# Seven-product FFN blocks for all 22 blocks of a hybrid decoder step, with no FFN block beside the sampled tokens

## The chip, the core and the metric

The kernel runs on one NeuronCore of a Trainium2 chip. The metric is the device time of one execution in microseconds (us). The engines are PE (TensorE, matrix products), DVE (VectorE), ACT (ScalarE), POOL (GpSimd) and SP (SyncE, which here only issues transfers). PE writes its results to PSUM banks; DVE or ACT read them from there. Each engine works through its own instructions in a fixed order, and so does each queue of transfers.

## What is computed

One layer of a decoder for a prompt of 1024 tokens and for 8 x 8 sampled tokens that have a past of 4096, 1024 channels wide, in float32. The token-mixing half has a short convolution, a dilated attention with six heads and a windowed attention. What matters here:

```
def apply_layer(x, mod, mixer, g_mix, g_ffn, w_out, w_gate_up, w_down):
    shift1, scale1, gate1, shift2, scale2, gate2 = mod
    mix, states = mixer(rmsnorm(x, g_mix) * (1 + scale1) + shift1)
    x = x + gate1 * (mix @ w_out)
    x = x + gate2 * swiglu(rmsnorm(x, g_ffn) * (1 + scale2) + shift2, w_gate_up, w_down)
    return x, states

def swiglu(h, w_gate_up, w_down):
    gate, up = jnp.split(h @ w_gate_up, 2, axis=-1)
    return (jax.nn.silu(gate) * up) @ w_down
```

The sampled tokens attend to a cache of 2048 keys and values for each of the 8 batches. The updated windows of these caches are outputs too, so most of the cache is copied from DRAM to DRAM as well.

## The kernel before

**Layout.** Channels lie on the 128 partitions, tokens on the free axis: 1088 columns, the prompt's 1024 and the sampled 64. The columns are split into three groups (`GRP`): 366, 366 and 356 columns; the sampled tokens are the end of the third. The FFN has 2816 hidden channels, 22 blocks of 128. A block needs a gate and an up product, 1024 channels deep each.

**Three matmuls for one.** float32 operands are split into a rounded high part and the rest (`halves` for weights, L85 to L93; `split_mix`, `second_norm` and `split_hid` for activations). `mm3` (L199) multiplies high by high, high by rest and rest by high. So a product of one block, one group and half the depth (512 channels, four chunks of 128) is 4 x 3 = 12 matmuls, and a full gate or up product of one group is 24. These are what the text calls large matmuls. ACT makes a weight's high part (L90), DVE or POOL its rest (L91).

**Seven products (Strassen's way, in Winograd's form).** `gate_up_2x2` (L968) treats gate and up for groups 0 and 1 as a 2 x 2 block product: weights are cut by gate/up and by half of the depth, activations by group and by half of the depth. Eight half-depth products become seven (7 x 12 = 84 large matmuls in place of 96). For that it needs four weight combinations for each block (t1 to t4, L972 to L975 on POOL) and, once for all blocks, four combinations of the activations, SA[1] to SA[4] (`sums_step`, L955, called four times: per call four additions on POOL, four on DVE, and the split of four results on ACT and DVE). Group 2 has no partner and stays at its 48 matmuls for a block. Before, 16 of the 22 blocks, 4 to 19, are done this way.

**Order of the work.** The program is written in stages; a scheduler then fixes each engine's order.
1. Modulation, norm, input projection, prompt attention.
2. The sampled tokens (`sample_steps`, L714): first three pairs of query heads of the windowed attention, then three pairs of heads of the dilated one, here called the first, second and third pair. Each of these streams 10 loads of 512 KB of keys and 10 of values from the cache (`stream_in`, L650), through seven buffers. Between its steps stands other work (`ahead_steps`, L879): the convolution projections, the output projection `w_out` (L754) for groups 0 and 1, their second norm, and FFN blocks 0 to 3 for groups 0 and 1 in the plain form (`gate_up`, L829, and `down_steps`, L860), with one modulation tile (`late_mod`, L355: four loads of 256 KB, 8 + 2 small matmuls) after each block. In FFN blocks 0 to 3 and in stage 1 state copies from DRAM to DRAM are issued on ACT's queue (`next_copy`, L103).
3. Pool `mid` (L915): the split of group 2's mix, `w_out` for group 2, its norm, and blocks 20 and 21 in the plain form for groups 0 and 1.
4. Pool `ffn` (L928): group 2 of blocks 0 to 3 with the four `sums_step` calls between them, their down product for group 2, group 2 of blocks 20 and 21 and their down products, then blocks 4 to 19 in pairs: two `gate_up_2x2`, then the down products of the pair. The last pair's down products are done by other column ranges (`LAST`), each followed by the final norm and the output transfers.

Group 2's output projection needs the sampled tokens' mix of all heads in the second half of its depth. PSUM has three buffers of the kind `ps_g`, which projections and down products use. Weights arrive in five buffers `wraw` and are split into four buffers `wsp`, all loaded by SP's one queue.

Of the kernel before, what the change touches and what calls it, by code (L numbers as in the profile page):

```python
# [15 lines left out]
KC = 8  # L16
# [14 lines left out]
FF_GROUPS = ((0, 4), (20, 2)) + tuple((f, 2) for f in range(4, 20, 2))  # L31
# [32 lines left out]
def _build(nc, tc, d, cst, rows, actp, stream, psum):  # L64
# [708 lines left out]
    def tmp():  # L773
        if "ff" in scratch:
# [85 lines left out]
    def down_steps(f0, hid, gs):  # L860
        if len(hid) == 4:
            for m in range(KC):
                w = wsel(split(d["w_dn"][f0 // 4, m]))
                for g in gs:
                    down(w, m, GRP[g], hid)
                yield
            return
        for q in range(4):
            w = wsel(split(d["w_d2"][f0 // 2 - 2, q]))
# [9 lines left out]
    def ahead_steps():  # L879
# [16 lines left out]
        flat = act_tile().rearrange("p h k c -> p (h k c)")  # L896
        hid = [flat[:, f * 1464:f * 1464 + 1464].rearrange("p (h c) -> p h c", h=2)
               for f in range(4)]
        for f0, nf in FF_GROUPS[:1]:
            for f in range(nf):  # L900
                gate_up(f0 + f, row("u_ff"), hid[f], (0, 1))
                late_mod(1)
                yield
            yield from down_steps(f0, hid[:nf], (0, 1))
# [7 lines left out]
    late_mod(16)  # L912
    samp.close()
    FE = FF_GROUPS[1][0]
    with tc.tile_pool(name="mid", bufs=1) as mid:  # L915
        scratch["ff"] = mid
        state["sub"] = 0
        mx[2] = mid.tile([128, 2, KC, 366], F32R, name="mx2")
        split_mix(2, mx[2])
        for m in range(KC):  # L920
            w_out(m, (2,))
        second_norm(2, second_rstd(2))
        first = [row("u_ff") for _ in range(NPRE)]
        for f, u in enumerate(first):
            gate_up(FE + f, u, None, (0, 1))

    early_pool.close()
    with tc.tile_pool(name="ffn", bufs=1, reuse_waits="tile") as ff:  # L928
        sums = ExitStack()
        sp_ = sums.enter_context(tc.tile_pool(name="sums", bufs=1, reuse_waits="tile"))  # L930
        scratch["ff"] = ff

        def hid_tile():
            return ff.tile([128, 2, T], F32R, tag="hid", bufs=2, name="hid")

        def tw():
            return sp_.tile([128, 512], F32, tag="tw", bufs=4, name="tw")
# [3 lines left out]
        N2 = GRP[0][1]  # L941
        SA = {i: sp_.tile([128, 2, 4, N2], F32R, name=f"sa{i}") for i in (1, 2, 4)}
        SA[3] = h2[1][:, :, 0:4, :]

        def whole(src, k):
            t = tw()[:, :N2]
            G.tensor_tensor(t, src[:, 0, k, :].bitcast(F32), src[:, 1, k, :].bitcast(F32), op=OP.add)
            return t

        def keep(i, k, t):  # L950
            hi, lo = SA[i][:, 0, k, :], SA[i][:, 1, k, :]
            S.activation(hi, t, AF.Copy)
            V.tensor_tensor(lo, t, hi.bitcast(F32), op=OP.subtract)

        def sums_step(k):  # L955

            a21, a22, a11 = whole(h2[1], k), whole(h2[1], k + 4), whole(h2[0], k)
            V.tensor_tensor(a22, a21, a22, op=OP.add)
            keep(1, k, a22)
            V.tensor_tensor(a21, a11, a21, op=OP.subtract)  # L960
            keep(3, k, a21)
            V.tensor_tensor(a11, a22, a11, op=OP.subtract)
            keep(2, k, a11)
            a12 = whole(h2[0], k + 4)
            V.tensor_tensor(a12, a12, a11, op=OP.subtract)
            keep(4, k, a12)

        def gate_up_2x2(f, hh):  # L968
            c2, n2 = GRP[2]
            b11, b12, b22, b21 = [load(d["w_gu"][f, n, hf]) for n, hf in ((0, 0), (1, 0), (1, 1), (0, 1))]  # L970
            t1, t2, t3, t4 = [tw() for _ in range(4)]
            G.tensor_tensor(t1, b12, b11, op=OP.subtract)  # L972
            G.tensor_tensor(t2, b22, t1, op=OP.subtract)
            G.tensor_tensor(t3, b22, b12, op=OP.subtract)
            G.tensor_tensor(t4, b21, t2, op=OP.subtract)  # L975
            u, uv = row("u"), row("uv")
            u2, u3 = uv[:, 0:N2], uv[:, N2:2 * N2]
            g0, g1, g2 = [u[:, c:c + n] for c, n in GRP]

            def product(ps, w, a, first):  # L980
                mm3(ps, w, [(k, k) for k in range(4)], a, N2, first=first, more=not first)

            def third(ps, w, half, first):
# [3 lines left out]
            w = wsel(halves(b11))  # L987
            pa, pg = ps_tile("s"), ps_tile("g")
            product(pa, w, lambda hl, k: h2[0][:, hl, k, :], True)
            S.activation(u2, pa[:, :N2], AF.Copy)  # L990
            third(pg, w, 0, True)
            pb = ps_tile("t")
            product(pb, wsel(halves(t2)), lambda hl, k: SA[2][:, hl, k, :], True)
            V.tensor_tensor(u2, u2, pb[:, :N2], op=OP.add)
            pd = ps_tile("s")
            product(pd, wsel(halves(t3)), lambda hl, k: SA[3][:, hl, k, :], True)
            V.tensor_tensor(u3, u2, pd[:, :N2], op=OP.add)
            w = wsel(halves(b21))
            product(pa, w, lambda hl, k: h2[0][:, hl, 4 + k, :], False)
            S.activation(g0, pa[:, :N2], AF.Silu)  # L1000
            third(pg, w, 1, False)
            ins = S.activation(g2, pg[:, :n2], AF.Silu)
            pe = ps_tile("t")
            product(pe, wsel(halves(t1)), lambda hl, k: SA[1][:, hl, k, :], True)
            V.tensor_tensor(u3, u3, pe[:, :N2], op=OP.add)
            product(pd, wsel(halves(t4)), lambda hl, k: h2[1][:, hl, 4 + k, :], False)
            V.tensor_tensor(g1, u2, pd[:, :N2], op=OP.add)
            S.activation(g1, g1, AF.Silu)
            V.tensor_tensor(g1, g1, u3, op=OP.mult)
            split_hid(u, hh, N2, N2)  # L1010
            w = wsel(halves(b22))
            product(pe, w, lambda hl, k: SA[4][:, hl, k, :], False)
            V.tensor_tensor(u2, u2, pe[:, :N2], op=OP.add)
            V.tensor_tensor(g0, g0, u2, op=OP.mult)
# [5 lines left out]
            split_hid(u, hh, c2, n2)  # L1020
            next_copy(ins)


        c2, n2 = GRP[2]
        for f0, nf in FF_GROUPS[:1]:
# [190 lines left out]
```

## Time and profile before

| | |
|---|---|
| median of 3 runs | 1411.46 us (1411.25 to 1416.62) |
| the profiled execution | 1411.32 us |
| its span, first to last instruction | 1409.5 us |
| PE busy, matmuls | 1353.3 us (96%), 9097 |
| DVE busy | 841.0 us (60%) |
| ACT busy | 582.5 us (41%) |
| POOL busy | 329.1 us (23%) |
| mean granted clock of PE | 0.982 |
| bytes moved by DMA | 190.81 MB |

A row of the profile names the line, the engine, the operation and the tiles (out<-in), then the time. `ps_` tiles are in PSUM, `wraw` is a loaded weight, `wsp` a split one, `raw` a piece of the cache, `tw` a scratch tile of the sums. A matmul's own duration overlaps with that of the next one, so its price is taken from the distance of starts: the number of matmuls in a window in which PE never waits.

### The profile page before, as it was taken

The page shows a single profiled execution, that of the slowest core. Times are in us where ns is not written, and L with a number is a line of the kernel's source. Part 1 is how long each engine was busy: PE and PEld are TensorE (multiplying, and loading weights), DVE is VectorE, ACT ScalarE, POOL GpSimd, SP SyncE. Part 2 cuts the span into 40 slices and gives each one's busy share as a digit, 9 for nine tenths or more (in the row PEclk, how much of TensorE's full clock was granted, in tenths as well). Part 3 has the DMA queues.
Part 4 walks back from the last instruction along what each step waited for, and adds up shares of the span by engine and source line. Part 5 has one row for each costly group of instructions (what it writes and reads, how often), then busy time and mean ns, then how long its engine had stood idle before and what let it go on. Part 6 is the DMA issues. An engine that isn't in the chain of part 4 may idle for free.

```text
span 1409.5 us, 23915 instructions
## 1 busy us (share of the span) xinstructions
PE 1353.3 (96%) x9097; PEld 1286.7 (91%) x9097; DVE 841.0 (60%) x1935; ACT 582.5 (41%) x1204; POOL 329.1 (23%) x364
## 2 busy tenths in 40 slices
PE   7999999999999998998998999999999999999994
PEld 5889999979898887888998999999999999999994
DVE  5468768265775326214569665757565666665657
ACT  5398764465654325222344413131313232322243
POOL 2143343233335220102015020202021111111114
PEclk9999999999999999999999999999999999999997
DMA  9342421452416679875333513141515142423103
GB/s 361 107 160 99 135 99 29 128 191 90 143 31 218 208 251 331 280 253 169 112 123 103 143 45 120 30 165 45 186 31 187 51 159 68 144 87 130 44 30 128
DMA packets 100804, 190.81 MB, mean 135 GB/s; under 512 B 14048, under 2 KB 51456, under 8 KB 100096
## 3 DMA queue, kind: packets, MB, share of 16 engines
q1 hardware_dynamic: 94112, 135.67, 30.1%
q10 hardware_dynamic: 6416, 53.55, 10.6%
q8 instruction: 72, 1.18, 0.3%
q14 instruction: 44, 0.36, 0.1%
q0 software_dynamic: 160, 0.04, 0.0%
HBM read 181.22 MB, written 59.23 MB: 171 GB/s over the span
## 4 chain that ended last, share of the span: by engine, by line
PE 83%; DMA 7%; DVE 4%; issue 2%; POOL 1%; ACT 1%; SPq 0%; POOLq 0%; ACTq 0%; DVEq 0%
PE ps_g L205 18%; PE ps_g L207 18%; PE ps_g L206 18%; PE ps_s L206 3%; PE ps_s L205 3%; PE ps_s L207 3%; DMA wraw<-in_w_gu 3%; PE ps_o L579 3%; PE ps_t L206 2%; PE ps_t L205 2%; PE ps_t L207 2%; PE ps_t L570 2%; DMA raw<-in_bv 1%; PE ps_g L180 1%; PE ps_s L528 1%
## 5 line engine op out<-in xcount | busy, mean ns | idle before, releaser
L205 PE MATMUL ps_g<-act,wsp 128*128 128x366 f32 (+1 forms) x1192 | 400.0, 337 | 5.5 <-ACT wsp L90 3.3
L207 PE MATMUL ps_g<-act,wsp 128*128 128x366 f32 (+1 forms) x1192 | 396.0, 333 | 4.0 <-DVE wsp L91 3.9
L206 PE MATMUL ps_g<-act,wsp 128*128 128x366 f32 (+1 forms) x1192 | 397.7, 334 | 0.4 <-DVE act L617 0.4
L90 ACT ACTIVATE wsp<-wraw 128x512 fp32r<-128x512 f32 x232 | 145.3, 629 | 270.5 <-PE ps_g L207 170.4
L205 PEld LDWEIGHTS ps_g<-act,wsp 128*128 128x128 f32 x1192 | 227.6, 191 | 13.0 <-issue 5.5
L207 PEld LDWEIGHTS ps_g<-act,wsp 128*128 128x128 f32 x1192 | 227.1, 191 | 9.2 <-DVE wsp L91 5.0
L91 DVE TENSOR_TENSOR wsp<-wraw,wsp 128x512 fp32r<-128x512 f32 x194 | 144.5, 745 | 146.3 <-ACT wsp L90 141.5
L206 PEld LDWEIGHTS ps_g<-act,wsp 128*128 128x128 f32 x1192 | 227.8, 191 | 4.0 <-issue 2.5
L205 PE MATMUL ps_g<-hid,wsp 128*128 128x366 f32 (+3 forms) x464 | 152.7, 331 | 4.6 <-DVE ts L767 3.6
L206 PE MATMUL ps_g<-hid,wsp 128*128 128x366 f32 (+3 forms) x464 | 152.3, 328 | 1.7 <-DVE hid L852 1.7
L207 PE MATMUL ps_g<-hid,wsp 128*128 128x366 f32 (+3 forms) x464 | 152.6, 329 | 0.0
L972 POOL TENSOR_TENSOR tw<-wraw 128x512 f32<-128x512 f32 x16 | 21.8, 1365 | 322.9 <-DMA wraw<-in_w_gu 157.0
L205 PEld LDWEIGHTS ps_g<-hid,wsp 128*128 128x128 f32 x464 | 87.6, 189 | 7.2 <-issue 3.6
L90 ACT ACTIVATE wsp<-tw 128x512 fp32r<-128x512 f32 x64 | 40.5, 633 | 122.5 <-PE ps_g L207 59.3
L206 PE MATMUL ps_s<-act,wsp 128*128 128x366 f32 x272 | 90.2, 332 | 0.0
L205 PE MATMUL ps_s<-act,wsp 128*128 128x366 f32 x272 | 90.1, 331 | 0.0
L206 PEld LDWEIGHTS ps_g<-hid,wsp 128*128 128x128 f32 x464 | 87.9, 189 | 2.5 <-DVE hid L852 2.3
L207 PE MATMUL ps_s<-act,wsp 128*128 128x366 f32 x272 | 89.9, 330 | 0.0
L91 POOL TENSOR_TENSOR wsp<-wraw,wsp 128x512 fp32r<-128x512 f32 x38 | 49.9, 1313 | 169.6 <-ACT wsp L90 158.0
L207 PEld LDWEIGHTS ps_g<-hid,wsp 128*128 128x128 f32 x464 | 87.8, 189 | 0.0
L763 DVE SCALAR_TENSOR_TENSOR p_qc<-ps_g,MOD,p_qc 128x366 f32<-128x366 f32 (+3 forms) x99 | 56.5, 572 | 39.9 <-PE ps_g L207 38.0
L763 DVE SCALAR_TENSOR_TENSOR p_q<-ps_g,MOD,p_q 128x366 f32<-128x366 f32 (+3 forms) x99 | 55.3, 570 | 38.5 <-PE ps_g L207 38.5
(346 smaller groups left out, 2453.3 us busy)
## 6 DMA issues: line engine op xcount, KB each, us to landing
wraw<-in_w_gu SPq DMA_DIRECT2D x112, 256.0 KB, 2.7
wraw<-in_wmod SPq DMA_DIRECT2D x64, 256.0 KB, 3.6
raw<-in_bk SPq DMA_DIRECT2D x30, 512.0 KB, 7.8
raw<-in_bv SPq DMA_DIRECT2D x30, 512.0 KB, 8.4
out_bk_b<-in_bk ACTq DMA_DIRECT2D x12, 1016.0 KB, 7.3
wraw<-in_w_in SPq DMA_DIRECT2D x36, 256.0 KB, 5.4
wraw<-in_w_d SPq DMA_DIRECT2D x36, 256.0 KB, 2.6
mraw<-in_wmod SPq DMA_DIRECT2D x32, 256.0 KB, 5.2
```

The source lines that it names most:

```text
L90: S.activation(sp[:, 0, :], raw, AF.Copy)
L91: (V if not state["sub"] or state["n"] % state["sub"] else G).tensor_tensor(sp[:, 1, :], raw, sp[:, 0, :].bitcast(F32), op=OP.subtract)
L180: ins = PE.matmul(ps[32 * q:32 * q + 32, :256], lhsT=csil[:, 4 * hf + q, :], rhs=raws[2 * hf + q // 2][:, q % 2 * 256:q % 2 * 256 + 256], ...
L205: PE.matmul(ps[:, :n], lhsT=w_hi, rhs=a(0, ak), start=first and j == 0, stop=False, **kw)
L206: PE.matmul(ps[:, :n], lhsT=w_hi, rhs=a(1, ak), start=False, stop=False, **kw)
L207: PE.matmul(ps[:, :n], lhsT=w_lo, rhs=a(0, ak), start=False, stop=last and j == m - 1, **kw)
L528: PE.matmul(ps[:, :sn], lhsT=QH[:, qsl], rhs=KS[hd][:, kk], start=True, stop=False)
L570: PE.transpose(pt[:, col:col + 128], Sb[:, (kb - k0) * 128:(kb - k0 + 1) * 128], ident)
L579: PE.matmul(po[:, q0:q0 + w], lhsT=Vt[:, kb, hd].rearrange("p a b -> p (a b)"), rhs=PT[:, hl, c0:c0 + w], start=fresh, stop=ch is chunks[- ...
L763: ins = V.scalar_tensor_tensor(x1[m][:, c0:c0 + k], ps[:, :k], MOD[:, gate + m, 0:1], x1[m][:, c0:c0 + k], op0=OP.mult, op1=OP.add)
L972: G.tensor_tensor(t1, b12, b11, op=OP.subtract)
```

## The change

All 22 blocks are done with seven products, and no FFN block stands beside the sampled tokens any more.

```
-FF_GROUPS = ((0, 4), (20, 2)) + tuple((f, 2) for f in range(4, 20, 2))
+FF_AHEAD = ()
+FF_PAIRS = (20,) + tuple(range(0, 20, 2))
...
         for m in range(KC):
             w_out(m, (0, 1))
+            late_mod(m % 2)
             yield
...
-        for f0, nf in FF_GROUPS[:1]:
-            for f in range(nf):
+        for f0 in FF_AHEAD:
...
+    mx[2] = act_tile()
+    split_mix(2, mx[2])
     samp.close()
...
-        mx[2] = mid.tile([128, 2, KC, 366], F32R, name="mx2")
-        split_mix(2, mx[2])
         for m in range(KC):
             w_out(m, (2,))
+            if m % 2:
+                sums_step(m // 2)
         second_norm(2, second_rstd(2))
         first = [row("u_ff") for _ in range(NPRE)]
         for f, u in enumerate(first):
-            gate_up(FE + f, u, None, (0, 1))
+            gate_up_2x2(FE + f, u, None)
...
-            next_copy(ins)
+        for _ in range(2 if f < 6 or hh is None else 1):
+            next_copy(ins)
```

- Blocks 20 and 21 come first for groups 0 and 1, now with seven products; `gate_up_2x2` takes the result row from its caller and leaves out group 2 where it gets no `hh` tile. Blocks 0 to 3 join the pairs. `down_steps` knows only pairs now, and the weights of all pairs lie in one array `w_dn`.
- The four modulation tiles that were left stand after every second block of `w_out`.
- Group 2's mix is split into a third big activation tile before the sampled tokens' pool is closed; the four `sums_step` calls stand between group 2's `w_out` blocks, and the pool of the sums is open until the end. The last norm's scratch lies in the memory of SA[1].
- The state copies that stood at blocks 0 to 3 go to the seven-product blocks: two at blocks 0 to 5 and in front for 20 and 21, one at the others.

The lines after L761 have moved by a few numbers in the new file: L655 there is the cache load of L653, L940 to L947 are the additions of the sums on DVE (L958 to L965 before), L935 the split of a sum (L953), L929 its additions on POOL (L947).

SP's queue, from the second pair's last values to the seventh of the third pair's values, before (`in_bk` are keys, `in_bv` values, `in_w_gu` FFN weights, `in_wmod` modulation weights):

```order
L653 DMA raw<-in_bv 128x4x256 x6
L653 DMA raw<-in_bk 128x4x256 x7
L97 DMA wraw<-in_w_gu 128x512 x3
L97 DMA wraw<-in_wmod 128x512 x4
L97 DMA wraw<-in_w_gu 128x512 x4
L97 DMA wraw<-in_wmod 128x512 x2
L653 DMA raw<-in_bk 128x4x256 x3
L97 DMA wraw<-in_wmod 128x512 x2
L97 DMA wraw<-in_w_gu 128x512
L653 DMA raw<-in_bv 128x4x256 x7
```

The same queue after, from the second pair's last keys on (`in_w_out` are the projection's weights, `in_xT` the third group's columns of the input):

```order
L99 DMA wraw<-in_w_out 128x512 x6
L655 DMA raw<-in_bk 128x4x256 x3
L655 DMA raw<-in_bv 128x4x256 x4
L99 DMA wraw<-in_w_out 128x512 x2
L655 DMA raw<-in_bv 128x4x256 x6
L655 DMA raw<-in_bk 128x4x256 x10
L759 DMA cv<-in_xT 128x356 x2
L759 DMA p_q_2101<-in_xT 128x356
L655 DMA raw<-in_bv 128x4x256
L759 DMA p_q_3212<-in_xT 128x356
```

Before, FFN and modulation weights stand between the third pair's loads; after, its keys follow the second pair's values at once, and its values stand behind the input's columns. From the first pair's first value to the second pair's last there were nine weight loads, and there are seventeen.

DVE's queue around the first of the sums, before (`act` is SA[3], which lies in an activation tile; `u_ff` is a row of block 20 or 21):

```order
L91 TENSOR_TENSOR wsp<-wraw,wsp 128x512
L958 TENSOR_TENSOR tw<-tw 128x366
L91 TENSOR_TENSOR wsp<-wraw,wsp 128x512
L960 TENSOR_TENSOR tw<-tw 128x366
L953 TENSOR_TENSOR sa_8244<-tw,sa_8244 128x366
L836 TENSOR_TENSOR u_ff<-u_ff,ps_g 128x366
L962 TENSOR_TENSOR tw<-tw 128x366
L953 TENSOR_TENSOR act<-tw,act 128x366
```

and after (`mixS` is the sampled tokens' mix, `cv` the first row of the projection's result; L765 and L769 are its evacuation):

```order
L708 COPY mixS<-ps_t 64x4x8 x4
L623 TENSOR_TENSOR act<-mixS,act 128x64
L940 TENSOR_TENSOR tw<-tw 128x366
L942 TENSOR_TENSOR tw<-tw 128x366
L935 TENSOR_TENSOR sa_6761<-tw,sa_6761 128x366
L944 TENSOR_TENSOR tw<-tw 128x366
L935 TENSOR_TENSOR act<-tw,act 128x366
L765 SCALAR_TENSOR_TENSOR cv<-ps_g,MOD,cv 128x292
L769 TENSOR_TENSOR ts<-ps_g,MOD 128x64
L947 TENSOR_TENSOR tw<-tw 128x366
L93 TENSOR_TENSOR wsp<-wraw,wsp 128x512
```

Before, the sums share DVE with blocks 0 to 3 and 20 and 21; after, they begin right behind the last copy of the sampled tokens' mix, and the projection's first evacuation stands behind five of them.

More of the change, by code (lines that the diff above doesn't have):

```diff
@@ L927, in _build @@
-    early_pool.close()
[L928 to L983, printed above, removed]
@@ new lines, in gate_up_2x2, with product, third @@
+    def gate_up_2x2(f, u, hh):
+        c2, n2 = GRP[2]
+        b11, b12, b22, b21 = [load(d["w_gu"][f, n, hf]) for n, hf in ((0, 0), (1, 0), (1, 1), (0, 1))]
+        t1, t2, t3, t4 = [tw() for _ in range(4)]
+        G.tensor_tensor(t1, b12, b11, op=OP.subtract)
+        G.tensor_tensor(t2, b22, t1, op=OP.subtract)
+        G.tensor_tensor(t3, b22, b12, op=OP.subtract)
+        G.tensor_tensor(t4, b21, t2, op=OP.subtract)
+        uv = row("uv")
+        u2, u3 = uv[:, 0:N2], uv[:, N2:2 * N2]
+        g0, g1, g2 = [u[:, c:c + n] for c, n in GRP]
+        def product(ps, w, a, first):
+            mm3(ps, w, [(k, k) for k in range(4)], a, N2, first=first, more=not first)
+        def third(ps, w, half, first):
+            if hh is not None:
@@ L1013, in gate_up_2x2 @@
[L1013 to L1014 removed]
+        w = wsel(halves(b11))
+        pa = ps_tile("s")
+        pg = ps_tile("g") if hh is not None else None
+        product(pa, w, lambda hl, k: h2[0][:, hl, k, :], True)
+        S.activation(u2, pa[:, :N2], AF.Copy)
+        third(pg, w, 0, True)
+        pb = ps_tile("t")
+        product(pb, wsel(halves(t2)), lambda hl, k: SA[2][:, hl, k, :], True)
+        V.tensor_tensor(u2, u2, pb[:, :N2], op=OP.add)
```

158 lines of the change are left out of this document (89 added, 69 removed).

## The prediction

> **What bounds the kernel now.** I read the page first, then the busy time by stage, then the tiles that mark where a stage begins, and last the queues of SP and DVE at two places.
>
> ```profile
> span 1409.5 us, 23915 instructions
> PE 1353.3 (96%) x9097; PEld 1286.7 (91%) x9097; DVE 841.0 (60%) x1935; ACT 582.5 (41%) x1204; POOL 329.1 (23%) x364
> PE 83%; DMA 7%; DVE 4%; issue 2%; POOL 1%; ACT 1%; SPq 0%; POOLq 0%; ACTq 0%; DVEq 0%
> ```
>
> PE is busy in 96% of the span and is 83% of the chain that ended last. So a product taken away is worth its time, as long as something is there to fill PE wherever it waits for a transfer. To see where that is, I cut the span at the first sampled scores, at the first product of the third group's output projection and at the first product after it that belongs to pair 20, 21 for the third group. The tiles give the first two cuts:
>
> ```profile
> L661 PE MATMUL ps_s<-raw,Q x288: 278/379/647, 450.7 to 595.6; 128*32 128x256 f32 x96, 128*32 128x136 f32 x24, 128*32 128x264 f32 x24
> L205 PE MATMUL ps_g<-mx,wsp x64: 320/325/329, 679.3 to 710.2; 128*128 128x356 f32 x64
> ```
>
> and the windows give each stage (columns: length, then busy time and count of PE, PEld, DVE, ACT, POOL, clock, DMA share, GB/s):
>
> ```profile
> 450.70:679.30 228.60, 214.25 (x1946) 189.83 (x1946) 80.82 (x194) 72.09 (x140) 39.46 (x58) 0.96 0.74 244
> 679.30:797.70 118.40, 114.35 (x686) 113.20 (x685) 85.76 (x186) 54.01 (x104) 28.52 (x29) 0.99 0.41 123
> 797.70:1409.50 611.80, 590.97 (x3546) 587.11 (x3544) 387.65 (x757) 181.71 (x329) 106.53 (x86) 0.99 0.29 98
> ...
> 975.00:1000.00 25.00, 25.00 (x153) 25.00 (x152) 15.83 (x30) 8.00 (x15) 3.83 (x3) 1.00 0.37 126
> ```
>
> The last row is plain FFN with the seven products: PE never idle, DVE at 63%, one product each 25.00 / 153 = 0.1634 us. The first row is another world: DMA is busy 74% of it, because the sampled tokens' keys and values stream through, and PE keeps going only because four FFN blocks lie beside them. The change takes exactly that cover away.
>
> **Saving: 11.8 us.** Six blocks (0 to 3, 20, 21) go from eight products of two groups to seven. One product is 12 matmuls, so 6 x 12 = 72 matmuls x 0.1634 = 11.8 us of PE. Down products stay the same in number; two pairs in place of one four-block group add 24 evacuations to DVE, hidden at 63%.
>
> The three stages hold 878, 672 and 3504 large matmuls by the program's order before, and 338, 324 and 4320 after (the sum falls by 72). Up to 450.7 us PE's order is the same in both, so I build the new time stage by stage from there.
>
> **Third stage.** 816 matmuls more than before at 0.1634 are 133.3 us: 611.8 + 133.3 = 745.1 us. The tail is the same work in other memory, costed at nothing. Of the 26 state copies on ACT's queue eight were beside the four FFN blocks of the sampled stage; they move into the second and third stage, where at a DMA share of 0.29 they are hidden.
>
> **First stage, A: when PE can go on with the third group's projection.** That needs the last sampled pair's output, so it needs its last values. Rows on the transfers:
>
> ```profile
> wraw<-in_wmod SPq DMA_DIRECT2D x64, 256.0 KB, 3.6
> raw<-in_bk SPq DMA_DIRECT2D x30, 512.0 KB, 7.8
> raw<-in_bv SPq DMA_DIRECT2D x30, 512.0 KB, 8.4
> ...
> wraw<-in_w_out SPq DMA_DIRECT2D x32, 256.0 KB, 2.7
> ...
> p_qc<-in_xT SPq DMA_DIRECT2D x3, 178.0 KB, 3.6
> ...
> raw<-in_cck SPq DMA_DIRECT2D x2, 256.0 KB, 4.4
> ```
>
> ```profile
> 446.70 3.07 SPq L653 DMA_DIRECT2D raw<-in_bk  x3
> 503.77 9.72 SPq L653 DMA_DIRECT2D raw<-in_bk  x7
> 542.38 9.65 SPq L653 DMA_DIRECT2D raw<-in_bk  x7
> ```
>
> ```profile
> 455.00:480.00 25.00, 25.00 (x276) 21.84 (x276) 8.86 (x27) 8.18 (x19) 8.37 (x16) 1.00 0.43 137
> ...
> 520.00:525.00 5.00, 5.00 (x40) 4.59 (x42) 2.24 (x4) 1.50 (x3) 0.00 (x0) 1.00 0.32 98
> 545.00:550.00 5.00, 5.00 (x65) 4.57 (x61) 3.69 (x8) 3.05 (x7) 0.00 (x0) 1.00 1.09 360
> ...
> 645.00:650.00 5.00, 5.00 (x37) 4.76 (x40) 0.60 (x1) 0.00 (x0) 0.00 (x0) 0.62 0.31 111
> ```
>
> ```profile
> 549.45 1.67 PE ps_o L695 x56
> ...
> 618.01 0.30 PE ps_g L207
> ...
> 649.06 0.17 PE ps_g L207
> ...
> 654.68 0.22 PE ps_t L701 x2
> ```
>
> When the queue is full it moves 360 GB/s. Before, the second pair's values are used up at 551 (549.45 + 1.67), and the third pair's first seven key loads have been issued at 542.38; the rest of that pair then waits behind FFN weights until 650. Now SP's queue has nothing of the FFN in between. From the first pair's first value to the second pair's last it carries 17 weight loads of 256 KB where it carried 9, 2.1 MB more, 5.8 us at 360 GB/s: 554 is my time for that point, a little less than 551 + 5.8, because the transfers had pauses there (below). Behind it come 20 loads of 512 KB, eight of 178 KB and three of 256 KB, 12.7 MB, 35.4 us: 589.5. From the last value to the split copy of the output there are products, an eviction, two transposes, four copies and a split. Before, L701 followed the products by 4 us with other work in between, and I take 4.5 us for the whole. A = 594.
>
> The four modulation tiles that used to lie beside the FFN blocks move into the first two groups' projection. Their matmuls and copies are the same; their 16 loads now stand on SP's queue in front of the first pair's keys and values. Up to 480 the transfers are busy 43% of the time, so the bytes (4.2 MB, 12 us) fit there. But a load of these needs one of five weight buffers, held until PE has used the tile before, and the keys are queued behind it: that is one reason for the upper bound below. The split of the third group's mix (16 copies on ACT, as many subtractions on DVE and POOL) moves ahead of the last pair and is hidden by PE's waiting; only its last column block is in the 4.5 us.
>
> Bounds of A: all 43.1 MB that SP is given from the first sampled load on (60 loads of 512 KB, 39 of 256, 8 of 178), at 360 GB/s without a pause, end 120 us after 446.70 and give A = 571. If the third pair's round takes as long as the second did (503.77 to 549.45, 45.7 us) and starts only at 554, its end is 600, and with xT and projection weights ahead of its values and the chain behind, A = 610. PE has 338 large matmuls (55 us) and the sampled products in 143 us, so it idles. Its clock falls in pauses (0.62 in the window at 645, products 0.30 apart at 618 and 0.17 at 649). That costs up to 3 us after a pause; I count it as covered by what follows.
>
> **Second stage, B: projection, sums and two blocks.** The sums for the seven products (L940 to L948, 16 additions on POOL, 16 on DVE, 16 splits) used to lie beside third-group products of four blocks; now they lie beside the projection, and DVE has them in its queue ahead of the projection's evacuations: PE, with three PSUM buffers for it, waits whenever an evacuation stands behind a sum. What they did before:
>
> ```profile
> 740.00:776.00 36.00, 32.14 (x184) 31.25 (x183) 33.65 (x53) 17.62 (x35) 18.76 (x15) 0.95 0.34 102
> ```
>
> ```profile
> 740.53 1.30 DVE L958 TENSOR_TENSOR tw<-tw 128x366 f32<-128x366 f32 x1 [2.07 <-POOL tw L947]
> 741.76 1.46 DVE L91 TENSOR_TENSOR wsp<-wraw,wsp 128x512 fp32r<-128x512 f32 x1
> 743.13 0.53 DVE L960 TENSOR_TENSOR tw<-tw 128x366 f32<-128x366 f32 x1
> ...
> 747.85 0.68 DVE L91 TENSOR_TENSOR wsp<-wraw,wsp 128x512 fp32r<-128x512 f32 x1
> ...
> 787.19 0.52 DVE L763 SCALAR_TENSOR_TENSOR cv<-ps_g,MOD,cv 128x292 f32<-128x292 f32 x1 [3.36 <-PE ps_g L207]
> 787.63 0.21 DVE L767 TENSOR_TENSOR ts<-ps_g,MOD 128x64 f32<-128x64 f32 x1
> ```
>
> DVE was busy 33.65 of 36 us and PE got 184 matmuls where 36 / 0.1634 would be 220. In the new place DVE holds 32 sums and splits at 0.53 (17.0 us), 10 weight splits at 0.68 (6.8) and 8 evacuations at 0.52 + 0.21 + 0.21 (7.5): 31.3 us. To that come the long forms (1.30 for 0.53, 1.46 for 0.68; ten such as before, 7.5 us) and POOL's first two additions: 41 us. PE has 156 matmuls (25.5 us) until then; the 168 matmuls of blocks 20 and 21 need the last sums and follow with 27.5 us. B = 68, beside a bare PE time of 324 x 0.1634 = 52.9, the lower bound. The third group's norm lies beside those 168.
>
> The upper bound of B comes from the long forms. In the rows below POOL's additions took from 0.962 to 3.249 us, and DVE's, with two inputs in SBUF, 0.53 or 1.30.
>
> ```profile
> L947 POOL TENSOR_TENSOR tw<-act x16: 962/1204/3249, 738.6 to 768.7; 128x366 f32<-128x366 f32 x16
> L958 DVE TENSOR_TENSOR tw<-tw x4: 526/910/1302, 740.5 to 766.9; 128x366 f32<-128x366 f32 x4
> ```
>
> Should the two engines take turns throughout, POOL's 16 x 0.962 = 15.4 us stand in place of my 7.5: B = 76. I keep 68, since most of DVE's rows stayed at 0.53. The Trainium skill's page "SBUF — State Buffer", section "Who interferes with whom", says that a DVE instruction with two SBUF inputs and a GpSimd instruction that reads SBUF exclude each other, and that the second blocks until the first is through. By that rule the sum is 1417 and not 1409; the trace agrees in part, with 1.30 for some and 0.53 for most.
>
> **The sum.** 594 + 68 + 745.1 = 1407.1 us of span. The profiled execution reports 1411.32 us, 1.8 more than its span, and the median of the three runs is 1411.46: I forecast 1409. Taken apart: beside its large matmuls at 0.1634 the first stage held 228.6 - 143.5 = 85.1 us, and will hold 143.3 - 55.2 = 88.1; the second 118.4 - 109.8 = 8.6, and will hold 68 - 52.9 = 15.1. These 9.5 us more are set against the 11.8 us saved.
>
> **The rivals.** About 0.5% (7 us) is what a measurement here can tell from no change: 1404.4 to 1418.5 is "same".
>
> 1. Forecast, both losses as priced: 1403 to 1418. Chance 0.34.
> 2. Faster: SP's queue has no FFN load and ACT's no state copy in the sampled stage any more, so the stream runs nearer its own floor. A = 583, half way between 571 and 594, and the sums find PE less bare, B = 64: 1394. For it: 1.09 DMA share at 545. Against: seven buffers hold the loads back. It decides below A + B = 657. Chance 0.34.
> 3. Slower: the third pair's keys, softmax and values come one after another as the second's did, with nothing for PE: A = 610, B = 68, 1425. For it: that round took 45.7 us before. Against: 36 projection matmuls and the split copies run beside it. It decides above A = 603. Chance 0.24.
> 4. POOL and DVE take turns in the sums: B = 76, 1417, at the upper edge of "same". Chance 0.05.
> 5. The change does not do what it says: a block of seven products is no cheaper, because its sums on DVE and POOL bind. Then 11.8 us are missing: 1421. Against: PE at 25.00 of 25.00 in the row at 975. Chance 0.03.
>
> **How the numbers follow.** Faster is case 2, 0.34. Same is cases 1 and 4 less a sliver, 0.38. Slower is cases 3 and 5 and that sliver, 0.28. The range takes in case 2 with its spread and most of case 3: 1389 to 1426.
>
> **What would show it.** In the new profile: the first projection product after the sampled tokens near 594 (case 2 near 583, case 3 near 610); PE's busy time from 450 to there well under its length with the DMA share over 0.8; DVE above 90% for some 40 us behind it, and the first pair product 20 some 41 us after; then 745 us to the end, with 153 matmuls per 25 us. Should the third stage be longer than 750, the moved work costs more than I say. Should PE's matmul count fall by other than 72, the saving is wrong.

## The result and the profile after

The changed kernel takes 1434.8 us (median of 4 runs, 1434.21 to 1438.65) against 1412.05 for the one before: a ratio of 1.0164, interval 1.0139 to 1.019. It is slower by 23 us, where 1409 was forecast and 1426 was the upper end. The profiled execution, of 1438.65 us, is the longest of the four; its span is 1436.9.

The head of its page, and the line of the chain by engine:

```profile
span 1436.9 us, 23814 instructions
PE 1353.0 (94%) x9025; PEld 1278.8 (89%) x9025; DVE 884.4 (62%) x2015; ACT 580.8 (40%) x1204; POOL 347.4 (24%) x376
PE 81%; DVE 8%; DMA 5%; issue 3%; ACT 2%; POOL 1%; SPq 0%; POOLq 0%; ACTq 0%; DVEq 0%
```

The 72 products are gone (9097 matmuls before, 9025 now), yet PE is busy for 1353.0 us where it was 1353.3. The 27.4 us by which the span is longer are idle time of PE. What the 72 products saved went to matmuls that now run at a lower clock: the mean granted clock is 0.968, and was 0.982.

The next four rows give the cuts of the forecast in the new trace: last sampled transposes, first product of the third group's projection, the first product of pair 20 (behind the norm's sums L802), and the first product that the third group has there.

```profile
606.88 0.69 PE L703 MATMUL ps_t<-ident,ob 128*128 128x128 f32 x2 [0.59 <-ACT ob L700]
608.55 0.66 PE L207 MATMUL ps_g<-act,wsp 128*128 128x356 f32 x1 [0.97 <-ACT act L622]
649.86 1.44 PE L802 MATMUL ps_t<-ones,acc 128*128 128x1 f32 x6 [11.42 <-DVE acc L799]
651.16 0.65 PE L207 MATMUL ps_t<-sa,wsp 128*128 128x366 f32 x1
...
689.29 0.33 PE L207 MATMUL ps_g<-act,wsp 128*128 128x356 f32 x1
```

and the windows between them, with the columns of the windows before (length; PE, PEld, DVE, ACT, POOL busy; clock, DMA share, GB/s):

```profile
450.70:608.55 157.85, 128.85 (x1410) 98.78 (x1408) 53.43 (x156) 49.06 (x102) 25.60 (x48) 0.87 0.82 268
608.55:689.29 80.74, 63.04 (x336) 60.16 (x337) 74.66 (x144) 38.75 (x76) 41.83 (x37) 0.87 0.31 99
689.29:1436.90 747.61, 728.34 (x4361) 724.72 (x4360) 471.56 (x919) 219.60 (x396) 126.00 (x102) 0.99 0.30 99
...
975.00:1000.00 25.00, 25.00 (x153) 24.97 (x152) 19.21 (x41) 4.56 (x8) 6.56 (x5) 1.00 0.16 55
```

So A = 608.55 (forecast 594), B = 80.74 (68), C = 747.6 (745.1). The plain FFN at 975 still makes 153 products in 25 us, and a product of the third stage takes as much busy time as before (728.34 us for 4320 of them, 590.97 for 3504: 0.169 us each): the loss lies in the two stages in front, where the clock is 0.87 and was 0.96 and 0.99. PE is idle for 29.0 us of the first stage and 17.7 of the second, where it was 14.35 and 4.05. The list of PE's waits names them:

```profile
PE ps_o L697 <- DMA raw<-in_bv: 11.7, 12, 1.6
PE ps_t L802 <- DVE acc L799: 11.4, 1, 11.4
PE ps_t L686 <- ACT SM L676: 8.1, 2, 5.6
PE ps_s L663 <- DMA raw<-in_bk: 7.0, 6, 4.5
```

Three of the four are sampled tokens that wait for values, softmax and keys. The second row is one wait of 11.4 us in stage B. What it waits for stands at the end of this piece of DVE's queue:

```profile
644.47 0.51 DVE L765 SCALAR_TENSOR_TENSOR p_qc<-ps_g,MOD,p_qc 128x292 f32<-128x292 f32 x1
...
646.11 1.28 DVE L770 TENSOR_TENSOR p_qc<-p_qc,ts 128x64 f32<-128x64 f32 x1
647.32 0.53 DVE L947 TENSOR_TENSOR tw<-tw 128x366 f32<-128x366 f32 x1
647.76 1.60 DVE L935 TENSOR_TENSOR sa<-tw,sa 128x366 fp32r<-128x366 f32 x1
649.29 0.52 DVE L799 TENSOR_TENSOR acc<-acc,tmp 128x356 f32<-128x356 f32 x1
```

PE ended the projection at 638.4. Its last product was taken out of PSUM only at 644.47, because DVE had sums and splits ahead of it; the norm's addition (L799) stood behind two more of them, at 649.29. And PE has the norm's L802 in its own queue ahead of pair 20. DVE is busy 41.61 of the first 42.6 us of this stage, as forecast, but the forecast had not seen that the norm hangs on the same queue and stands before the products that were to follow.

### The profile page after: what moved, and what is told of

The parts are those of the page before. It is cut to its first block, busy times and chain, and to the rows that moved or that the text cites. A ratio compares the mean times of both kernels' runs of the same rounds, so it can differ in the third digit from the quotient of the medians.

```text
span 1436.9 us, 23814 instructions
## 1 busy us (share of the span) xinstructions
PE 1353.0 (94%) x9025; PEld 1278.8 (89%) x9025; DVE 884.4 (62%) x2015; ACT 580.8 (40%) x1204; POOL 347.4 (24%) x376
## 4 chain that ended last, share of the span: by engine, by line
PE 81%; DVE 8%; DMA 5%; issue 3%; ACT 2%; POOL 1%; SPq 0%; POOLq 0%; ACTq 0%; DVEq 0%
PE ps_g L207 16%; PE ps_g L208 16%; PE ps_g L209 16%; PE ps_s L207 4%; PE ps_s L208 4%; PE ps_s L209 4%; PE ps_t L208 3%; PE ps_t L207 3%; PE ps_t L209 3%; PE ps_o L581 2%; PE ps_t L572 2%; DMA raw<-in_bv 2%; DMA raw<-in_bk 2%; DVE wsp L93 1%; PE ps_g L182 1%
## 5 line engine op out<-in xcount | busy, mean ns | idle before, releaser
L207 PE MATMUL ps_g<-act,wsp 128*128 128x366 f32 (+1 forms) x1000 | 335.0, 336 | 4.2 <-DVE u L330 2.4
L208 PE MATMUL ps_g<-act,wsp 128*128 128x366 f32 (+1 forms) x1000 | 331.9, 332 | 0.5 <-DVE act L619 0.5
L209 PE MATMUL ps_g<-act,wsp 128*128 128x366 f32 (+1 forms) x1000 | 330.2, 331 | 1.6 <-DVE wsp L93 1.5
L92 ACT ACTIVATE wsp<-wraw 128x512 fp32r<-128x512 f32 x206 | 129.1, 629 | 236.5 <-PE ps_g L209 141.0
L207 PEld LDWEIGHTS ps_g<-act,wsp 128*128 128x128 f32 x1000 | 190.1, 191 | 12.5 <-issue 5.4
L93 DVE TENSOR_TENSOR wsp<-wraw,wsp 128x512 fp32r<-128x512 f32 x180 | 134.0, 745 | 106.2 <-ACT wsp L92 101.5
L209 PEld LDWEIGHTS ps_g<-act,wsp 128*128 128x128 f32 x1000 | 189.7, 190 | 5.1 <-DVE wsp L93 3.3
L208 PEld LDWEIGHTS ps_g<-act,wsp 128*128 128x128 f32 x1000 | 190.0, 190 | 3.7 <-issue 1.9
L207 PE MATMUL ps_g<-hid,wsp 128*128 128x366 f32 (+2 forms) x528 | 173.4, 331 | 3.7 <-DVE ts L769 3.2
L208 PE MATMUL ps_g<-hid,wsp 128*128 128x366 f32 (+2 forms) x528 | 174.3, 330 | 1.6 <-DVE hid L857 1.5
L209 PE MATMUL ps_g<-hid,wsp 128*128 128x366 f32 (+2 forms) x528 | 173.8, 329 | 0.0
L207 PE MATMUL ps_s<-act,wsp 128*128 128x366 f32 x368 | 122.5, 333 | 3.2 <-ACT u_ff L985 2.2
L208 PE MATMUL ps_s<-act,wsp 128*128 128x366 f32 x368 | 122.1, 332 | 0.0
L209 PE MATMUL ps_s<-act,wsp 128*128 128x366 f32 x368 | 121.6, 331 | 0.0
L955 POOL TENSOR_TENSOR tw<-wraw 128x512 f32<-128x512 f32 x22 | 30.3, 1379 | 373.8 <-DMA wraw<-in_w_gu 223.7
L92 ACT ACTIVATE wsp<-tw 128x512 fp32r<-128x512 f32 x88 | 55.6, 632 | 155.0 <-PE ps_g L209 72.9
L207 PEld LDWEIGHTS ps_g<-hid,wsp 128*128 128x128 f32 x528 | 99.7, 189 | 5.5 <-issue 3.4
L208 PEld LDWEIGHTS ps_g<-hid,wsp 128*128 128x128 f32 x528 | 99.8, 189 | 2.8 <-DVE hid L857 2.8
L209 PEld LDWEIGHTS ps_g<-hid,wsp 128*128 128x128 f32 x528 | 99.8, 189 | 0.0
L765 DVE SCALAR_TENSOR_TENSOR p_qc<-ps_g,MOD,p_qc 128x366 f32<-128x366 f32 (+3 forms) x108 | 61.6, 571 | 54.6 <-PE ps_g L209 52.2
L207 PE MATMUL ps_t<-sa,wsp 128*128 128x366 f32 x264 | 88.2, 334 | 0.0
L208 PE MATMUL ps_t<-sa,wsp 128*128 128x366 f32 x264 | 88.0, 333 | 0.0
```

What stands on the lines that cost most here:

```text
L92: S.activation(sp[:, 0, :], raw, AF.Copy)
L93: (V if not state["sub"] or state["n"] % state["sub"] else G).tensor_tensor(sp[:, 1, :], raw, sp[:, 0, :].bitcast(F32), op=OP.subtract)
L207: PE.matmul(ps[:, :n], lhsT=w_hi, rhs=a(0, ak), start=first and j == 0, stop=False, **kw)
L208: PE.matmul(ps[:, :n], lhsT=w_hi, rhs=a(1, ak), start=False, stop=False, **kw)
L209: PE.matmul(ps[:, :n], lhsT=w_lo, rhs=a(0, ak), start=False, stop=last and j == m - 1, **kw)
L765: ins = V.scalar_tensor_tensor(x1[m][:, c0:c0 + k], ps[:, :k], MOD[:, gate + m, 0:1], x1[m][:, c0:c0 + k], op0=OP.mult, op1=OP.add)
```

## The experiments

Theory 1: both losses are of order, not of work. The sampled tokens' transfers lost the products that covered them, and the sums stand on DVE ahead of the projection and the norm. The rivals: the sums cost nothing and only the sampled stage lost; the modulation tiles or the number of buffers hold the stream back; blocks of seven products save nothing.

**Cover put back.** Two kernels with one or two pairs ahead for the first two groups, as the tables allow:

```
-FF_AHEAD = ()
-FF_PAIRS = (20,) + tuple(range(0, 20, 2))
+FF_AHEAD = (0,)                # two pairs: (0, 2)
+FF_PAIRS = (20,) + tuple(range(2, 20, 2))   # (20,) + tuple(range(4, 20, 2))
```

> As the changed kernel, but four FFN blocks (two pairs) are again ahead of the third group for the first two groups; blocks 20 and 21 keep the seven products, beside the sums. Theory 1 (both halves of the loss: the sampled tokens lost the products that covered their transfers, and the sums stand on DVE ahead of the projection and of the norm): the third group's projection starts near 683 us, about where it did before (679), but the stretch from there to the end of blocks 20 and 21 for the first two groups is about 82 us as in the changed kernel; 1426 us in all. Rival (only the sampled stage lost, the sums are innocent): that stretch is 66 us and the time 1410. Rival (the modulation tiles beside the projection cost the sampled stage its time): the projection starts 8 us or more later than 683.

> As the changed kernel, but one FFN pair (blocks 0, 1) is ahead for the first two groups. By the order, 590 large products stand beside the sampled tokens where 338 did. Theory 1 (lost cover): these 252 products, 41 us of TensorE, cost the sampled stage only 28 us: the third group's projection starts near 637 us in place of 608.6, the stretch behind it stays 82 us, and the whole is 1423 us. Rival (TensorE is not short of work there, the products only come on top): 650 us and 1437.

(The products come out of the order: 338 beside the sampled tokens in the changed kernel, 590 with one pair and 878 with two, as many as before the change. In both, all 192 products of the third group's projection come behind the sampled tokens, where the changed kernel ran 36 of them beside the third pair.) Measured: two pairs 1433.25 us (ratio 1.0159, interval 1.0114 to 1.0203), one pair 1428.15 (1.0118, 1.0076 to 1.0159), 7 and 5 us above the price of theory 1; where these come from was not followed up. First the rows of one pair, then of two: first projection product, norm, first product of pair 20, first product behind the stretch.

```profile
628.93 0.59 PE L207 MATMUL ps_g<-act,wsp 128*128 128x356 f32 x2 [0.52 <-ACT act L622]
680.56 1.44 PE L802 MATMUL ps_t<-ones,acc 128*128 128x1 f32 x6 [11.76 <-DVE acc L799]
681.86 0.65 PE L207 MATMUL ps_t<-sa,wsp 128*128 128x366 f32 x1
...
716.65 0.32 PE L207 MATMUL ps_g<-act,wsp 128*128 128x356 f32 x1
```

```profile
679.33 0.60 PE L207 MATMUL ps_g<-act,wsp 128*128 128x356 f32 x2 [0.68 <-ACT act L622]
728.43 1.44 PE L802 MATMUL ps_t<-ones,acc 128*128 128x1 f32 x6 [11.40 <-DVE acc L799]
...
765.27 0.33 PE L207 MATMUL ps_g<-act,wsp 128*128 128x356 f32 x1
```

252 products, 41.2 us of PE, moved the projection's start by 628.93 - 608.55 = 20.4 us: half of them ran in time that was lost in the changed kernel. With two pairs the projection starts at 679.33, where it started before the change (679.3) with as many products, so the modulation tiles in their new place cost nothing there. The stretch behind it stays long (87.7 and 85.9 us; the changed kernel's 80.7 and the 36 products more, 5.9 us, are 86.6), with the same wait of over 11 us for `acc` whatever stands in the sampled stage. The two losses are separate.

**The sums left out, and moved.** In the first kernel the calls of `sums_step` are gone and the seven products read parts of the unsummed activations in place of the sums. In the second each plain block, 20 and 21, is followed by two of the calls. The first cut below is common to both kernels; the second cut is of the second kernel alone.

```
         for m in range(KC):
             w_out(m, (2,))
-            if m % 2:
-                sums_step(m // 2)
...
-            gate_up_2x2(FE + f, u, None)
+            gate_up(FE + f, u, None, (0, 1))
+            for k in range(2):
+                sums_step(2 * f + k)
```

> As the changed kernel, with the sums and their splits left out (16 additions on POOL, 32 instructions on DVE, 16 on ACT); the seven products run on unsummed parts, so the output isn't the reference's. Theory 1 (DVE's queue of sums delays the projection's evacuations and with them the norm): from the first projection product to the end of blocks 20 and 21 for the first two groups 66 us in place of 80.7; 1421 us. Rival (the norm's chain of small steps, bare on TensorE's queue, is what costs): 80 us stays, 1435.

> As the changed kernel, with blocks 20 and 21 as plain products for the first two groups, as before the change, and the sums called behind the third group's norm, beside these 192 products. Theory 1: projection and norm run without sums ahead of them, and the stretch from the first projection product to the last of blocks 20 and 21 is 69 us in place of 80.7, although it holds 24 products more; 1424 us. Rival (sums beside plain blocks stop TensorE as much): 75 to 80 us, 1431 to 1435.

In the second kernel block 21 reads, for the second group, activations over which block 20's sums were partly written, so its output isn't the reference's either. Measured: 1425.92 us without sums (1.0106, 1.0052 to 1.0159), 1417.05 with late ones (1.0046, 1.0025 to 1.0068). Without sums the stretch is 676.06 - 607.28 = 68.8 us, 12 less than with them, and the wait for `acc` is halved:

```profile
607.28 0.96 PE L207 MATMUL ps_g<-act,wsp 128*128 128x356 f32 x2 [0.97 <-ACT act L622]
640.33 1.44 PE L802 MATMUL ps_t<-ones,acc 128*128 128x1 f32 x6 [5.10 <-DVE acc L799]
...
676.06 0.33 PE L207 MATMUL ps_g<-act,wsp 128*128 128x356 f32 x1
```

With the plain blocks it is 667.22 - 605.55 = 61.7 us, and so shorter than without any sums, although 24 products more stand in it. The order allows this: plain blocks 20 and 21 need no sums, and PE has 37 of their products in its queue ahead of the norm's L802. So the sums cost 12 us of the stretch, and the rival that sums beside plain blocks stop PE as much falls. The rival that the norm's chain is bare falls only in part: without the sums 5.10 us of its wait stay, and they go when plain products stand ahead of it.

The same move with the sums later still, two by two behind the third group's products of blocks 20 and 21.

```
                 if FE <= f < FE + NPRE:
                     u = first[f - FE]
                     split_hid(u, hh, 0, GRP[2][0])
                     gate_up(f, u, hh, (2,))
+                    for k in range(2):
+                        sums_step(2 * (f - FE) + k)
```

> As the changed kernel, with blocks 20 and 21 as plain products for the first two groups, and the sums called two by two behind the third group's gate and up products of blocks 20 and 21, when every plain product that reads the unsummed activations has been issued; it computes the whole reference. Theory 1 (sums ahead of the projection and the norm on DVE cost the second stretch): as with the sums beside the plain blocks, some 62 us for projection, norm and the two blocks, and 1417 us. Rival (in the new place they stop the first pair of seven products, which waits for the last sum): 1424 us or more.

Measured: 1417.12 us (1.0036, 1.0022 to 1.0049). In the stretch PE is busy in all 61.16 us, and the norm's matmuls no longer wait:

```profile
608.72:669.88 61.16, 61.16 (x360) 61.16 (x361) 50.64 (x117) 31.49 (x63) 21.98 (x25) 0.96 0.38 118
```

```profile
642.50 0.72 PE L802 MATMUL ps_t<-ones,acc 128*128 128x1 f32 x6
```

**The projection dealt out.** With no work added, the first two groups' projection is spread over two sampled pairs:

```
-    for _ in sample_steps():
-        for _ in range(2):
+    for i, _ in enumerate(sample_steps()):
+        for _ in range((2, 1, 1, 2, 1, 1, 2, 2, 2)[i]):
             next(ahead, None)
```

> As the changed kernel, with the first two groups' projection dealt out over the first and second sampled pair (2, 1, 1, 2, 1, 1, 2, 2, 2 steps behind the nine sampled steps, where it was 2 behind each); no work is added or taken away. Theory 1 (the sampled tokens' transfers want products beside them at the right time): the last sampled transposes come near 590 us where they came at 607, and the time is 1420 us. Rival (the transfers set the end whatever stands beside them, since seven buffers hold the stream): 605 us and 1434.

> Both: the projection dealt out over two sampled pairs, and the sums behind the plain blocks 20 and 21. If the two losses are separate, their savings add: 1402 us, some 10 below the kernel before. If the dealing out is worth nothing: 1417.

Measured: alone 1421.44 us (1.0075, 1.0048 to 1.0102); with the sums of the last experiment 1403.44 us (0.9937, 0.9921 to 0.9953). Two windows of the changed kernel, then two of the dealt-out one and its last transposes:

```profile
455.00:480.00 25.00, 25.00 (x270) 21.91 (x262) 8.66 (x29) 9.89 (x22) 8.10 (x15) 1.00 0.49 158
530.00:608.00 78.00, 50.92 (x623) 32.37 (x621) 31.33 (x89) 27.07 (x56) 4.60 (x14) 0.74 0.85 276
```

```profile
455.00:480.00 25.00, 23.07 (x274) 17.26 (x273) 7.99 (x27) 7.61 (x17) 7.61 (x15) 1.00 0.90 298
480.00:580.00 100.00, 85.52 (x1025) 66.69 (x1024) 37.62 (x99) 32.15 (x60) 11.12 (x17) 0.90 0.91 302
```

```profile
580.02 0.69 PE L703 MATMUL ps_t<-ident,ob 128*128 128x128 f32 x2 [0.65 <-ACT ob L700]
```

In the changed kernel PE is full at first while the transfers stand at 0.49, and later the transfers are at 0.85 while PE is busy 50.9 of 78 us. Dealt out, both go on together (0.90 and 0.91), and the sampled tokens end 27 us earlier, at 580 (theory 1 had 590, and the bytes gave the forecast a floor of 571 for A). In the two profiled executions the third group's projection starts 28 us earlier (580.50), the stretch behind it is 5.4 us longer (86.09), since the 36 products that ran beside the third pair, 5.9 us, now come behind it, and the last stage is 1.2 us longer (748.81): the spans differ by 21.5. By the medians the whole gains 13.4 us; those two executions are the changed kernel's slowest and this one's fastest, and this kernel's five executions spread over 13 us. The two mends add within that spread: 17.7 alone, 13.4 alone, 31.4 together. The kernel with both beats the one before the change by 0.6% (interval 0.5 to 0.8). Its stages:

```profile
450.70:585.19 134.49, 115.95 (x1374) 89.67 (x1373) 48.45 (x142) 43.49 (x86) 22.29 (x43) 0.94 0.90 298
585.19:653.79 68.60, 67.62 (x396) 66.32 (x397) 58.57 (x131) 36.52 (x80) 26.40 (x29) 0.98 0.45 138
653.79:1398.60 744.81, 728.18 (x4361) 725.14 (x4360) 478.75 (x931) 222.05 (x403) 131.21 (x106) 0.99 0.30 100
```

Its executions took 1400.09 to 1406.07 us, and the profiled one is at the lower end, so 1403.4 is the number to compare.

**One pair ahead, with the sums beside its third group.** Blocks 20 and 21 are plain, and `sums_step` is called twice behind each third-group block of the pair that was ahead.

> One FFN pair ahead for the first two groups as cover (28.15 us were lost less there than it holds in products), blocks 20 and 21 plain, the sums beside the third group's products of the pair that was ahead, much as in the kernel before but with one pair where it had four blocks. Theory 1: projection from 629 us, 70 us from there to the end of blocks 20 and 21, and 1415 us; if the sums beside the third group's products cost as before the change (36 products fewer in 36 us) it is 1419.

(The 28.15 in this text is a slip; the measured figure is the 20.4 us above.) Measured: 1408.4 us (0.9983, 0.9963 to 1.0003), better than either price, and no different from the kernel before. The projection starts at 628.66 and the stretch behind it takes 71.4 us, as priced; so it is the last stage that the price of 1415 had too long, and the cost of sums beside the third group's products, the reason for 1419, does not show.

**Rivals on the sampled stage and on the saving.** The last four, each a change of one thing:

```
+            if len(mods) < 4:
+                one = load(d["wmod"][t, 0], stream, "wraw", RAWB)
+                mraw[t] = [one] * 4
+            else:
...
-HRAW = 7
+HRAW = 6
...
-                    gate_up_2x2(f, row("u"), hh)
+                    gate_up(f, row("u"), hh, range(3)) if f < 4 else gate_up_2x2(f, row("u"), hh)
...
-        for _ in range((2, 1, 1, 2, 1, 1, 2, 2, 2)[i]):
+        for _ in range((2, 1, 1, 1, 1, 2, 2, 2, 2)[i]):
```

> As the changed kernel, but each of the four modulation tiles beside the projection loads one quarter of its weights and uses it four times: 12 of 16 loads (3.1 MB) are left out, so these modulation values are wrong; matmuls and copies stay. Theory 1 (the sampled tokens lack products at the right time): the loads had room, the last sampled transposes stay at 603 to 607 us, 1431 to 1435 us. Rival (these loads stand in front of the keys and values on SP's queue and cost the second pair its 12 us): 595 us and 1423.

Measured: 1435.91 us (1.0175, 1.0138 to 1.0213), last transposes at 602.57, 4.3 us earlier. In the five kernels that leave the sampled stage as it is (the one with four plain blocks, below, among them) these transposes come between 603.89 and 609.64, so the loads in front of the keys cost a few us at most, and only 1.3 us lie outside that spread. The time shows none of it, and the rival falls.

> As the changed kernel, with six buffers for the sampled keys and values in place of seven (there is no memory for eight). Theory 1 (products are missing, the depth of the stream matters little): the last sampled transposes at most 3 us later, 1438 us. Rival (the buffers hold the stream back in every round): 9 us or more later, 1444 us.

Measured: 1439.19 us (1.0188, 1.0156 to 1.0221), last transposes at 607.74, 0.9 us later and within the same spread. One buffer fewer does not hold the stream back, so the seven were not what held it in every round; whether more would help was not tried.

> As the kernel with the sums behind the plain blocks 20 and 21 (1417 us), but blocks 0 to 3 take the plain way for all three groups, on activations whose first half in the second group is by then overwritten by a sum, so the output isn't the reference's. It adds 48 products. Theory 1 (a block of seven products is cheaper by its products, 12 x 0.1634 us a block): 1417 + 7.8 = 1425 us. Rival (the sums of its weights on POOL and DVE take the saving back): 1417.

Measured: 1426.7 us (1.0109, 1.0081 to 1.0136), 9.6 us above the 1417.1 without this edit. A block of seven products is worth its products; the 1.8 us above 7.8 are no more than executions of one kernel differ by.

> As the kernel with both mends (1403 us), with the projection dealt out a little later: 2, 1, 1, 1, 1, 2, 2, 2, 2 steps. If the third pair still lacks products: 1398 us. If the stream is the bound by now: 1403 or a little more, as the norms of the first two groups come later.

Measured: 1402.87 us (0.9944, 0.992 to 0.9968), the same as before the edit; the last transposes come 7 us later, at 590.68. More cover for the third pair gains nothing here.

## Why the prediction was wrong

**A, 594 forecast, 608.55 measured.** The step that failed is "554 is my time for that point", the end of the second pair's values. ACT takes the products out when they end (L700), for the three pairs at:

```profile
518.71 0.47 ACT L700 ACTIVATE ob<-ps_o,stb 128x256 f32<-128x256 f32 x1 [8.78 <-PE ps_o L697]
566.77 0.47 ACT L700 ACTIVATE ob<-ps_o,stb 128x256 f32<-128x256 f32 x1 [2.76 <-PE ps_o L697]
606.35 0.47 ACT L700 ACTIVATE ob<-ps_o,stb 128x256 f32<-128x256 f32 x1 [17.65 <-PE ps_o L697]
```

566.8, then, not 554: 12.8 of the 14.6 us that A is late. I took the kernel before's time for that point and added the 2.1 MB of eight more weight loads, as if they only passed through a full queue. The windows of the kernel before, then two of the changed one, and the issue of the second pair's last three keys in both:

```profile
446.70:551.00 104.30, 97.74 (x1062) 83.25 (x1060) 39.93 (x109) 38.69 (x73) 24.45 (x42) 0.97 0.81 266
446.70:551.00 104.30, 94.55 (x933) 77.78 (x931) 33.67 (x96) 31.52 (x64) 21.70 (x40) 0.95 0.82 267
551.00:567.00 16.00, 10.57 (x193) 8.23 (x193) 11.92 (x31) 8.31 (x15) 0.00 (x0) 0.79 0.74 227
...
525.19 1.90 SPq L653 DMA_DIRECT2D raw<-in_bk  x3
535.48 1.89 SPq L655 DMA_DIRECT2D raw<-in_bk  x3
```

By 551 as much had been moved as before the change, so the pace that I took over held until then. But those keys were issued 10 us later, behind six of the projection's weight loads, and from 551 to 567 the transfers moved 227 GB/s where I had counted 360, while PE waited for softmax and values. The dealt-out kernel shows that the order of the work beside the stream, and not the bytes, set the time: with the projection elsewhere, the first window of its stream stands at 0.90 in place of 0.49, and its second pair ends at 536.2. The modulation loads, which I named as a reason for the upper bound, account for a few us of A at most, by the spread above. The rest of the slip isn't taken apart further: PE's wait of 5.6 us for the second pair's softmax, which stands on DVE behind the norms of the first two groups, is in it, but no run removed that wait alone, and the dealt-out kernel has one of the same length in its third pair. From the second pair's end on the forecast nearly held: 35.4 + 4.5 us were allowed, 38.0 passed to PE's last wait for a value (604.78) and 3.8 more to the first projection product.

**B, 68 forecast, 80.74 measured, outside its bounds (52.9 to 76).** The failed step is "168 matmuls ... follow with 27.5 us". The sums were sized rightly, 41 us until pair 20's first product against 42.6. But the 168 products took 38.1 us. They stand behind the norm in PE's queue, the norm behind the sums in DVE's, so its small steps came last and bare: waits of 1.7 us for the norm's root and of 2.2 and 1.0 for u_ff and uv; and after the wait of 11.42 us the products came at nearly half their pace until about 660 (granted clock 0.50 from 651.16 to 660). Three rows from then and three from after it, with the starts 0.306 and 0.167 us apart:

```profile
653.06 0.51 PE L209 MATMUL ps_t<-sa,wsp 128*128 128x366 f32 x1
653.37 0.51 PE L207 MATMUL ps_t<-sa,wsp 128*128 128x366 f32 x1
653.67 0.51 PE L208 MATMUL ps_t<-sa,wsp 128*128 128x366 f32 x1
...
660.62 0.33 PE L209 MATMUL ps_s<-act,wsp 128*128 128x366 f32 x1
660.79 0.33 PE L207 MATMUL ps_s<-act,wsp 128*128 128x366 f32 x1
660.96 0.33 PE L208 MATMUL ps_s<-act,wsp 128*128 128x366 f32 x1
```

The Trainium skill's page "TensorE: Matmul & The Clock Gate", Part 1, says that the array is granted half its clock after some 3.4 us of idleness; the row of 11.42 us and the spacing, 1.8 times as wide, agree with it. "I count it as covered by what follows" was wrong in B: nothing covered it.

"The third group's norm lies beside those 168" was the sentence that the program's own order refutes: in PE's rows L802 stands before the first `sa` product, and the step that waits for the root (L806) behind only 12 of them.

**C, 745.1 forecast, 747.6 measured.** Right, with the copies on ACT's queue in it; the 2.5 us lie within what the price of a product leaves open, 0.1634 in the row at 975 and 0.169 over the whole stage, for 816 products.

**The saving.** 11.8 us forecast; four plain blocks cost 9.6 where 7.8 was expected. Right. But PE's busy time did not fall by it, since products of the first two stages ran at the lower clock.

**The rivals.** Case 3 had A's value, 610, but another way to it: it let the third round take 45.7 us from 554, where it took 39.6 from 566.8. That the number fits was luck. Case 4, POOL and DVE taking turns in the sums, was truer in its mechanism than its chance of 0.05, though its B of 76 was passed for another reason, the norm and the clock. POOL's and DVE's additions in the sums:

```profile
L929 POOL TENSOR_TENSOR tw<-act x16: 958/1269/1489, 607.8 to 642.8; 128x366 f32<-128x366 f32 x16
L935 DVE TENSOR_TENSOR sa<-tw,sa x12: 522/528/1601, 612.2 to 649.7; 128x366 fp32r<-128x366 f32 x12
L940 DVE TENSOR_TENSOR tw<-tw x4: 842/1122/1304, 609.8 to 641.4; 128x366 f32<-128x366 f32 x4
```

Summed over DVE's queue from 609 to 651, 22 of 52 instructions with two SBUF inputs were long, by 14.2 us in all; I had 7.5 and the case 15.4. Each of the 22 overlaps an addition on POOL by over 0.1 us, and so do 11 of the 30 that stayed short: the two engines took turns often, but not throughout. The 41 us came out right because another part was too large: DVE's instructions follow each other before the one ahead has ended, 0.45 us apart for 0.53 of duration (612.21, 612.66, 613.11 for three of them), so counting durations overstates a full queue. Case 5 falls by the run with four plain blocks, case 2 did not come.

**The chance.** 0.28 was given to slower, and no case let both terms be late at once; A + B missed by 27 us. The experiments show the two losses to be separate, so nothing kept them from coming together.

## What to carry to other kernels

When work that covered a stream of transfers is taken away, the other engines' queues must be gone through again from that point: what stands behind the new work on the vector engine, and what the tensor engine has in its own queue ahead of the products that are to fill the gap. Moving work (sums behind two blocks that were made plain again, at the price of 24 products, and a projection dealt out over the stream) brought 31 us here, nearly three times what the saved products were worth. A number for a point in time may be taken over from another program only if what stands ahead of that point stays the same; else the stage is to be built from both the transfers' and the tensor engine's side.

## What the runs showed of the hardware

The idle tensor engine is paid twice: PE's busy time stayed at 1353 us with 72 products fewer, since products behind waits ran at up to 0.306 us in place of 0.167 (granted clock 0.50 behind the wait of 11.42 us). And a queue of short DVE instructions moves by 0.45 us for each row of 0.53 (612.21, 612.66, 613.11). Where such instructions with two inputs in SBUF ran beside additions on POOL, 22 of 52 took up to 1.60 us.
